# Encoder layer in one kernel: the decay products of the state-space part, from unrounded 128-column products to rounded two-part products of 128 and 64 columns

## Chip, cores and metric

The kernel runs on one core of a Trainium2 chip. The time is the device time of one execution in microseconds (us); below, a run is one such execution and the median of several is given. Less is better.

## What is computed

One encoder layer over 256 tokens of width 2048: a combined input projection, three branches (a bidirectional state-space scan, a dilated window attention, a convolution module), their gated sum, an output projection and an MLP. The change touches the state-space branch alone, and in it the product that the reference calls `y_diag`, in chunks of 128 tokens, 32 heads of 64 channels, 4 groups of 8 heads, in both directions:

```python
lmat = jnp.exp(jnp.where(lower, seg, -jnp.inf))
cb = jnp.einsum("bclgn,bcsgn->bgcls", cc, bc)
y_diag = jnp.einsum("bgrcls,bcsgrp->bclgrp", cb[:, :, None] * lmat, xdt)
...
y = y_fwd + y_bwd + d_skip[:, None] * xh
```

For one chunk and one head this is a 128x128 matrix (decay times `cb` times `dt`, both directions added) times a 128x64 block of x.

## The kernel before

**The stream of weights.** All large products are cut into blocks of up to 512 output columns, and each block into units of 256 rows of its weight. There are 696 units, counted here from 0. For unit k, SyncE loads a tile `raw`, ScalarE (ACT) rounds it to `hi` (L1211), VectorE (DVE) forms the rest `lo` (L255), and TensorE (PE) multiplies `hi` and `lo` with the two parts of the activations into a PSUM tile `main` (L1264 to L1276). `hi` and `lo` have four buffers each, `raw` five, `main` two. The loop at the end of the kernel issues, for each k, the split of unit k+3, then the products of unit k, then whatever side work fits in.

**Side work.** Everything else is a job: a generator that says before each step what it needs. "v", "a", "g" and "p" are planned nanoseconds on DVE, ACT, GpSimd and PE; "b" is a PSUM bank (of 4); "m" asks for slabs, the 4 KB-per-partition tiles that all jobs share (`SLOTS`, 33 of them); "w" lets some units pass; "j" waits for another job's result. `Sched.tick` gives each engine some planned time per unit, and jobs are tried in order of priority: 0 for those that read a `main` and so free it, 1 for conv and output parts, 2 for attention, 3 for the state-space jobs (`job_cb`, `job_ssd`), 4 for the long convolution. A job that asks for slabs that aren't free waits.

**What forces an order.** Before the first product of a block, `mm` asks `S.require` that the block two before it has been read, since there are two `main` tiles. If it hasn't, `require` runs jobs without regard to planned time, by rising priority, until it has:

```python
S.require(lambda: id(j) in st["main_free"], f"block {bi - 2} read")
...
for j in [x for x in self.jobs if x.prio <= level]:
    while not cond() and not j.done and self._try(j, True):
        moved = True
```

All that these jobs issue then stands, on every engine, ahead of the block's first unit. In the program before this happens once, at unit 28, with two steps.

**The state-space jobs.** `job_ssd(g, c)` serves 8 heads of group g and chunk c; there are eight such jobs, and two of a group can be open at once. It takes four slabs: `rh`, `rl` (the masked decay increments, rounded and rest), `em` and `xsx`. After an off-diagonal part (L811 to L825) it goes twice through a half of four heads. A half issues, in this order: masks scaled by the increments on ACT and DVE (L832, L835), four products that sum them (L842), `cb` scaled by dt (L846, L854), the exponential (L849), their product (L857), the head products (L864) and the addition to `y` (L869). L864 takes x for two heads at once, so of its 128 columns the half that belongs to the other head is thrown away by the strided read at L867.

Of the kernel before, what the change touches and what calls it, by code (L numbers as in the profile page):

```python
# [12 lines left out]
F32 = mybir.dt.float32  # L13
F32R = mybir.dt.float32r
BF16 = mybir.dt.bfloat16
AF = mybir.ActivationFunctionType
ALU = mybir.AluOpType
# [3 lines left out]
P = 128  # L21
# [169 lines left out]
def kernel(ctx: ExitStack, tc: tile.TileContext, xT, xn, par, cm, cd, cq, w1, wq, ws, out):  # L191
    nc = tc.nc
    S = Sched()
# [11 lines left out]
    def nm(s):  # L205
        cnt[0] += 1
        return f"{s}_{cnt[0]}"

    def slab(shape, dt=F32, name="s"):
        return gp.tile([P] + list(shape), dt, tag="g", name=nm(name))  # L210

    def bank(shape=(512,), name="b"):
        return pd.tile([P] + list(shape), F32, tag="d", name=nm(name))
# [4 lines left out]
    V, A, G, PE = nc.vector, nc.scalar, nc.gpsimd, nc.tensor  # L218
# [11 lines left out]
    def par_(k, i=0, n=1):  # L230
        o = _OFF[k][0] + i
        return cpar[:, o:o + n]
# [563 lines left out]
    def job_ssd(g, c):  # L796

        yield "j", lambda: cbs[g] is not None
        dt, adh, adl, sp = st["dt"], st["adh"], st["adl"], st["sp"]
        yield "m", 4  # L800
        rh = slab([2, 4, P], F32R, name="rh")
        rl = slab([2, 4, P], F32R, name="rl")
        em = slab([2, 4, P], name="em")
        xsx = slab([2, 512], name="xsx")
        cb, x, yy = cbs[g], xs[g], y[g][:, c, :]
        o = 1 - c
        sS = sp[:, 0 if c == 1 else 2, 8 * g:8 * g + 8]
        sP = sp[:, 1 if c == 1 else 3, 8 * g:8 * g + 8]
        v8 = lambda ap: ap.rearrange("p (h e) -> p h e", h=8)
        yield "v", 620  # L810
        V.tensor_tensor(v8(xsx[:, 0, :]), v8(x[:, o, :]), sS[:, :, None].to_broadcast([P, 8, 64]), op=ALU.mult)  # L811
        yield "g", 1200
        G.tensor_tensor(v8(xsx[:, 1, :]), v8(x[:, c, :]),
                        par_("dsk", 8 * g, 8)[:, :, None].to_broadcast([P, 8, 64]), op=ALU.mult)
        yield "b", 1
        bo = bank()
        yield "w", 1
        yield "p", 860
        PE.matmul(bo, cb[:, 4 + c, :], xsx[:, 0, :], start=True, stop=True)  # L819
        yield "w", 1  # L820
        yield "v", 620
        V.tensor_tensor(v8(yy), v8(bo), sP[:, :, None].to_broadcast([P, 8, 64]), op=ALU.mult)
        S.banks += 1
        yield "v", 620
        V.tensor_tensor(yy, yy, xsx[:, 1, :], op=ALU.add)  # L825
        for hb in range(2):
            for d in range(2):
                for i in range(4):
                    col = 32 * d + 8 * g + 4 * hb + i
                    msk = LE if d == 0 else GE  # L830
                    yield "a", 290
                    A.activation(rh[:, d, i, :], msk, AF.Copy, scale=adh[:, c, col:col + 1].bitcast(F32))  # L832
                col = 32 * d + 8 * g + 4 * hb
                yield "v", 620
                V.tensor_tensor(rl[:, d], msk[:, None, :].to_broadcast([P, 4, P]),  # L835
                                adl[:, c, col:col + 4][:, :, None].to_broadcast([P, 4, P]), op=ALU.mult)
            yield "w", 1
            yield "b", 1
            ba = bank((4, P))
            yield "p", 900  # L840
            for n, (lt, src) in enumerate(((gtr, rh[:, 0]), (gtr, rl[:, 0]), (ltr, rh[:, 1]), (ltr, rl[:, 1]))):
                PE.matmul(ba, lt, src, start=(n == 0), stop=(n == 3))  # L842
            for i in range(4):
                yield "a", 290
                col = 8 * g + 4 * hb + i
                A.activation(em[:, 1, i, :], cb[:, c, :], AF.Copy, scale=dt[:, c, col:col + 1])  # L846
            yield "w", 1
            yield "a", 500
            A.activation(em[:, 0], ba, AF.Exp)  # L849
            S.banks += 1  # L850
            for i in range(4):
                yield "v", 270
                col = 32 + 8 * g + 4 * hb + i
                V.scalar_tensor_tensor(em[:, 1, i, :], cb[:, 2 + c, :], dt[:, c, col:col + 1], em[:, 1, i, :],  # L854
                                       op0=ALU.mult, op1=ALU.add)
            yield "v", 620
            V.tensor_tensor(em[:, 0], em[:, 0], em[:, 1], op=ALU.mult)  # L857
            yield "w", 1
            yield "b", 1
            bd = bank((4, P))  # L860
            yield "p", 880
            for i in range(4):
                pr = 256 * hb + 128 * (i // 2)
                PE.matmul(bd[:, i, :], em[:, 0, i, :], x[:, c, pr:pr + P], start=True, stop=True)  # L864
            yield "w", 1
            yield "v", 400
            bv = bd.rearrange("p (q r) e -> p q (r e)", q=2).rearrange("p q (s e) -> p q s e", s=4)[:, :, 0::3, :]  # L867
            yv = yy[:, 256 * hb:256 * hb + 256].rearrange("p (q s e) -> p q s e", q=2, s=2)
            V.tensor_tensor(yv, yv, bv, op=ALU.add)  # L869
            S.banks += 1  # L870
        S.give(4)
        st["ssd_c"][g] += 1
        st["ssd_n"] += 1
        if st["ssd_c"][g] == 2:
            S.give(2)
            if g == 3:
                S.give(2)
# [242 lines left out]
    def xbc_block(i):  # L1120
        def post(m):
            js = [(job_xbc(m, i, (16, 20, 0, 4, 8, 12)[i]), 1)]
            if i >= 2:
                js += [(job_cb(i - 2), 3), (job_ssd(i - 2, 0), 3), (job_ssd(i - 2, 1), 3)]
            return js
        block("W", "h", post)
# [37 lines left out]
    for o in ORDER:  # L1164
        k, i = o[0], int(o[1])
# [235 lines left out]
```

## Time and profile before

| what | value |
|---|---|
| median of 3 runs | 1981.73 us (1981.35 to 1984.19) |
| the profiled execution | 1983.86 us |
| its span | 1982.1 us |
| DVE busy | 1309.0 us, 66% of the span |
| ACT busy | 1036.0 us, 52% of the span |
| granted TensorE clock, mean | 0.999 |
| state-space halves on the chip | first L842 at 298.5 us, last L869 at 741.1 us |

The profile page gives the busy time of each engine, then groups of instructions by source line; a group's row says what it writes and reads, how often it ran, its busy time, the mean time of one, and how long its engine sat idle before it and for whom. PE is one queue of products with a queue of weight loads (PEld) beside it. A PE product's listed time includes its way through the array, so products overlap; what one costs is read from the distance of two starts.

### The profile page before, as it was taken

The page shows a single profiled execution, that of the slowest core. Times are in us where ns is not written, and L with a number is a line of the kernel's source. Part 1 is how long each engine was busy: PE and PEld are TensorE (multiplying, and loading weights), DVE is VectorE, ACT ScalarE, POOL GpSimd, SP SyncE. Part 2 cuts the span into 40 slices and gives each one's busy share as a digit, 9 for nine tenths or more (in the row PEclk, how much of TensorE's full clock was granted, in tenths as well). Part 3 has the DMA queues.
Part 4 walks back from the last instruction along what each step waited for, and adds up shares of the span by engine and source line. Part 5 has one row for each costly group of instructions (what it writes and reads, how often), then busy time and mean ns, then how long its engine had stood idle before and what let it go on. Part 6 is the DMA issues. An engine that isn't in the chain of part 4 may idle for free.

```text
span 1982.1 us, 29949 instructions
## 1 busy us (share of the span) xinstructions
PE 1966.0 (99%) x11798; PEld 1766.0 (89%) x11798; DVE 1309.0 (66%) x1847; ACT 1036.0 (52%) x1446; POOL 47.5 (2%) x42
## 2 busy tenths in 40 slices
PE   8999999999999999999999999999999999999999
PEld 7999999999998888888888888999988998998887
DVE  5778887887887889896654555555555554455443
ACT  6654576777757655545654444544443443344332
POOL 0000010000000000003000000000000000000000
PEclk9999999999999999999999999999999999999999
DMA  8555554554554555555555556555555555555554
GB/s 284 184 175 183 165 185 145 167 172 144 184 170 161 176 181 178 183 191 187 190 191 183 189 189 207 194 186 192 188 190 189 189 191 191 188 186 191 190 181 149
DMA packets 105342, 364.51 MB, mean 184 GB/s; under 512 B 11760, under 2 KB 12272, under 8 KB 105200
## 3 DMA queue, kind: packets, MB, share of 16 engines
q1 hardware_dynamic: 103904, 360.23, 55.4%
q10 hardware_dynamic: 1296, 2.36, 0.3%
q8 instruction: 92, 1.51, 0.3%
q14 instruction: 50, 0.41, 0.1%
HBM read 360.45 MB, written 2.10 MB: 183 GB/s over the span
## 4 chain that ended last, share of the span: by engine, by line
PE 95%; DVE 0%; issue 0%
PE main L1273 19%; PE main L1274 19%; PE main L1276 19%; PE main L1266 11%; PE main L1264 11%; PE main L1268 11%; PE b L842 1%; PE b L864 1%; PE b L968 1%; PE b L1273 0%; PE b L1274 0%; PE b L1276 0%; PE b L819 0%; PE b L501 0%; PE b L757 0%; PE b L742 0%
## 5 line engine op out<-in xcount | busy, mean ns | idle before, releaser
L255 DVE TENSOR_TENSOR lo<-raw,hi 128x1024 fp32r<-128x1024 f32 (+2 forms) x697 | 831.5, 1194 | 643.5 <-ACT hi L1211 638.7
L1211 ACT ACTIVATE hi<-raw 128x1024 fp32r<-128x1024 f32 (+2 forms) x695 | 716.2, 1032 | 868.7 <-PE main L1274 487.8
L1273 PE MATMUL main<-hi,hh 128*128 128x512 f32 (+1 forms) x800 | 306.1, 383 | 0.0
L1274 PE MATMUL main<-hi,hl 128*128 128x512 f32 (+1 forms) x800 | 299.0, 374 | 0.0
L1266 PE MATMUL main<-x2l,hi 128*128 128x256 f32 x1024 | 246.4, 281 | 0.0
L1264 PE MATMUL main<-x2h,hi 128*128 128x256 f32 x1024 | 246.3, 279 | 0.0
L1266 PE MATMUL main<-hl,hi 128*128 128x256 f32 x896 | 216.3, 281 | 3.2 <-DVE hl L255 3.2
L1264 PE MATMUL main<-hh,hi 128*128 128x256 f32 x896 | 217.7, 282 | 0.0
L565 DVE SCALAR_TENSOR_TENSOR co<-cin,cpar,co 128x256 f32<-128x256 f32 x480 | 211.1, 491 | 0.0
L1276 PE MATMUL main<-lo,hh 128*128 128x512 f32 (+1 forms) x800 | 200.5, 372 | 0.0
L1264 PEld LDWEIGHTS main<-x2h,hi 128*128 128x128 f32 x1024 | 192.7, 188 | 0.2
L1266 PEld LDWEIGHTS main<-x2l,hi 128*128 128x128 f32 x1024 | 192.6, 188 | 0.2
L1273 PE MATMUL main<-hi,ah 128*128 128x512 f32 x480 | 188.9, 394 | 0.0
L1274 PE MATMUL main<-hi,al 128*128 128x512 f32 x480 | 188.6, 393 | 0.0
L1273 PEld LDWEIGHTS main<-hi,hh 128*128 128x128 f32 x800 | 152.5, 191 | 23.4 <-ACT hi L1211 1.2
L1274 PEld LDWEIGHTS main<-hi,hl 128*128 128x128 f32 x800 | 152.2, 190 | 22.9 <-issue 1.9
L1266 PEld LDWEIGHTS main<-hl,hi 128*128 128x128 f32 x896 | 168.8, 188 | 4.2 <-DVE hl L255 3.6
L1264 PEld LDWEIGHTS main<-hh,hi 128*128 128x128 f32 x896 | 169.2, 189 | 0.6
L1276 PEld LDWEIGHTS main<-lo,hh 128*128 128x128 f32 x800 | 148.0, 190 | 22.1
L1268 PE MATMUL main<-x2h,lo 128*128 128x256 f32 x1024 | 138.3, 277 | 0.0
L1276 PE MATMUL main<-lo,ah 128*128 128x512 f32 x480 | 130.1, 393 | 0.0
L1268 PEld LDWEIGHTS main<-x2h,lo 128*128 128x128 f32 x1024 | 127.6, 188 | 0.0
(244 smaller groups left out, 2304.5 us busy)
## 6 DMA issues: line engine op xcount, KB each, us to landing
raw<-ws_dram SPq DMA_DIRECT2D x600, 512.0 KB, 3.3
raw<-wq_dram SPq DMA_DIRECT2D x88, 384.0 KB, 3.1
raw<-w_dram SPq DMA_DIRECT2D x7, 448.0 KB, 7.0
xr<-xn_dram SPq DMA_DIRECT2D x4, 512.0 KB, 9.2
x<-xn_dram SPq DMA_DIRECT2D x4, 512.0 KB, 4.3
xt<-xT_dram SPq DMA_DIRECT2D x7, 256.0 KB, 7.0
out_dram<-x SPq DMA_DIRECT2D x4, 256.0 KB, 3.7
out_dram<-x ACTq DMA_DIRECT2D x4, 256.0 KB, 5.6
```

Source lines behind the costliest of these rows:

```text
L255: V.tensor_tensor(lo, raw, hi.bitcast(F32), op=ALU.subtract)
L565: V.scalar_tensor_tensor(dst[:, e, :], x[:, e, k:k + T], par_("dw", (2 * i + e) * 31 + k), dst[:, e, :], op0=ALU.mult, op1=ALU.add)
L842: PE.matmul(ba, lt, src, start=(n == 0), stop=(n == 3))
L864: PE.matmul(bd[:, i, :], em[:, 0, i, :], x[:, c, pr:pr + P], start=True, stop=True)
L968: PE.transpose(b[:, e, t * P:t * P + P], src[:, t, k * P:k * P + P], ID)
L1211: A.activation(h, r, AF.Copy)
L1264: PE.matmul(o, wh[:, e, cs], ah, start=(first and e == 0 and c % 2 == 0), stop=False, skip_group_check=True)
L1266: PE.matmul(o, wh[:, e, cs], al, start=False, stop=False, skip_group_check=True)
L1268: PE.matmul(o, wl[:, e, cs], ah, start=False, stop=(last and e == 1), skip_group_check=True)
L1273: PE.matmul(o, ah[:, xs_], wh[:, e, :], start=(first and e == 0), stop=False)
L1274: PE.matmul(o, al[:, xs_], wh[:, e, :], start=False, stop=False)
L1276: PE.matmul(o, ah[:, xs_], wl[:, e, :], start=False, stop=(last and e == 1))
```

## The change

The head products are no longer made from unrounded operands. x of the chunk is split once per job into a rounded part and a rest, which stand side by side per head in a new slab `xhl` (128 columns per head). The matrix `em` is split in the same way into `rh[:, 0]` and `rh[:, 1]`, the slab that held the masked increments until then. Per head there are two products in the rounded format: the rounded matrix with both parts of x (128 columns), and the rest of the matrix with the rounded part of x (64 columns). The product of the two rests is left out. The two column halves are then added to `y` one after the other. A job now asks for five slabs instead of four; the number of slabs stays 33.

```diff
-        yield "m", 4
+        yield "m", 5
+        xhl = slab([8, 2, 64], F32R, name="xhl")
...
+        yield "a", 500
+        A.activation(xhl[:, :, 0, :], v8(x[:, c, :]), AF.Copy)
+        yield "w", 1
+        yield "v", 620
+        V.tensor_tensor(xhl[:, :, 1, :], v8(x[:, c, :]), xhl[:, :, 0, :].bitcast(F32), op=ALU.subtract)
...
             yield "w", 1
+            yield "a", 500
+            A.activation(rh[:, 0], em[:, 0], AF.Copy)
+            yield "w", 1
+            yield "v", 620
+            V.tensor_tensor(rh[:, 1], em[:, 0], rh[:, 0].bitcast(F32), op=ALU.subtract)
+            yield "w", 1
             yield "b", 1
             bd = bank((4, P))
-            yield "p", 880
+            yield "p", 480
             for i in range(4):
-                pr = 256 * hb + 128 * (i // 2)
-                PE.matmul(bd[:, i, :], em[:, 0, i, :], x[:, c, pr:pr + P], start=True, stop=True)
+                PE.matmul(bd[:, i, :], rh[:, 0, i, :], xhl[:, 4 * hb + i].rearrange("p a e -> p (a e)"), start=(i == 0),
+                          stop=False, skip_group_check=True)
+                PE.matmul(bd[:, i, 0:64], rh[:, 1, i, :], xhl[:, 4 * hb + i, 0, :], start=False, stop=(i == 3),
+                          skip_group_check=True)
             yield "w", 1
-            yield "v", 400
-            bv = bd.rearrange("p (q r) e -> p q (r e)", q=2).rearrange("p q (s e) -> p q s e", s=4)[:, :, 0::3, :]
-            yv = yy[:, 256 * hb:256 * hb + 256].rearrange("p (q s e) -> p q s e", q=2, s=2)
-            V.tensor_tensor(yv, yv, bv, op=ALU.add)
+            yv = yy[:, 256 * hb:256 * hb + 256].rearrange("p (i e) -> p i e", i=4)
+            for a in range(2):
+                yield "v", 400
+                V.tensor_tensor(yv, yv, bd[:, :, 64 * a:64 * a + 64], op=ALU.add)
             S.banks += 1
-        S.give(4)
+        S.give(5)
```

The planner therefore sets the side work in another order. In the changed program, the jobs' free slabs fall to 0 at unit 120, 1 at unit 176 and 0 at unit 242, and at these places a job that has to read a `main` waits for slabs (or stands behind one that does), so `require` runs the state-space jobs to their end. The lines of the changed program are moved: L838 is L832 of before, L841 is L835, L848 is L842, L852 is L846, L855 is L849, L860 is L854, L863 is L857, L965 is L951, L1225 is L1211. New are L828 and L831 (the parts of x), L866 and L869 (those of the matrix), L875 and L877 (the products) and L883 (the two additions).

The first place is ACT between the units 179 and 181 of the changed program; unit 176 is the first of the block of attention values. `hi` is the rounded weight, `qn` the normalised queries, read from a `main`, and the numbers behind the names are the tiles' own. These are the last rows ahead of the rounding of unit 180:

```order
L866 ACTIVATE rh_5796<-em_5798 128x512
L828 ACTIVATE xhl_5884<-xs_5689 128x8x64
L838 ACTIVATE rh_5885<-cmask,adh 128x128 x8
L852 ACTIVATE em_5887<-cb_5786,dt 128x128 x4
L855 ACTIVATE em_5887<-b_5907 128x512
L866 ACTIVATE rh_5885<-em_5887 128x512
L838 ACTIVATE rh_5885<-cmask,adh 128x128 x8
L852 ACTIVATE em_5887<-cb_5786,dt 128x128 x4
L855 ACTIVATE em_5887<-b_5945 128x512
L866 ACTIVATE rh_5885<-em_5887 128x512
L489 ACTIVATE qn_5973<-main_5271,qrs_5479 128x128 x6
L1225 ACTIVATE hi_5998<-raw_5638 128x768
```

In the program before, ACT reads the same block's `main` in these rows:

```order
L1211 ACTIVATE hi_5756<-raw_5684 128x768
L459 ACTIVATE junk_5732,ss_5731<-main_5477 128x128 x2
L763 ACTIVATE oh_828<-b_5737 128x2x128
L1211 ACTIVATE hi_5783<-raw_5712 128x768
L270 ACTIVATE rs_803_5800<-qms_5774 128x6
L1211 ACTIVATE hi_5808<-raw_5754 128x768
L489 ACTIVATE qn_5829<-main_5477,qrs_5775 128x128 x4
L1211 ACTIVATE hi_5837<-raw_5781 128x768
```

What stood before between the roundings of many units now stands in one piece between those of units 179 and 180: after the rounding of unit 179 come six squares, two copies of x, seven copies of `em` (five of them with the masks, scaled copies and exponential of a whole half ahead of them), two parts of x, and last the six `qn`.

The second place is DVE around the units 242 to 250, where the attention's projections are multiplied by their gates (L965, before L951) and so read. In the changed program, after the forced half of a state-space job:

```order
L869 TENSOR_TENSOR rh_7787<-em_7789,rh_7787 128x512
L883 TENSOR_TENSOR y_6947<-y_6947,b_7864 128x256 x2
L255 TENSOR_TENSOR lo_7895<-raw_7748,hi_7894 128x1024
L255 TENSOR_TENSOR lo_7914<-raw_7769,hi_7913 128x1024
L965 TENSOR_TENSOR mg_7891<-main_7730,sg_6818 128x512 x2
L255 TENSOR_TENSOR lo_7935<-raw_7892,hi_7934 128x1024
L255 TENSOR_TENSOR lo_7954<-raw_7911,hi_7953 128x1024
L965 TENSOR_TENSOR mg_7910<-main_7878,sg_7028 128x512 x2
```

and before:

```order
L255 TENSOR_TENSOR lo_7727<-raw_7669,hi_7726 128x1024
L951 TENSOR_TENSOR mg_7715<-main_7675,sg_6761 128x512 x2
L854 SCALAR_TENSOR_TENSOR em_7503<-cb_6818,dt,em_7503 128x128
L255 TENSOR_TENSOR lo_7750<-raw_7697,hi_7749 128x1024
L854 SCALAR_TENSOR_TENSOR em_7503<-cb_6818,dt,em_7503 128x128 x3
L857 TENSOR_TENSOR em_7503<-em_7503 128x512
L255 TENSOR_TENSOR lo_7773<-raw_7724,hi_7772 128x1024
L951 TENSOR_TENSOR mg_7765<-main_7730,sg_6982 128x512 x2
```

Each `lo` row is the split of one unit. Before, the gate product of the block that ends with unit 241 stands behind the split of unit 245; now it stands behind that of unit 247, and those of the next two blocks have moved two splits back in the same way.

## Prediction

> **What bounds the kernel now.** First the page's head, then who waits for whom.
>
> ```profile
> span 1982.1 us, 29949 instructions
> PE 1966.0 (99%) x11798; PEld 1766.0 (89%) x11798; DVE 1309.0 (66%) x1847; ACT 1036.0 (52%) x1446; POOL 47.5 (2%) x42
> ```
>
> PE is busy 99% of the span. The list of waits, PE's own, has five rows in all:
>
> ```profile
> PE b L296 <- DVE dg L291: 4.1, 1, 4.1
> PE main L1266 <- DVE hl L255: 3.2, 2, 2.2
> PE main L1273 <- ACT hi L1211: 2.9, 2, 2.1
> PE b L1288 <- DVE ones L236: 1.1, 1, 1.1
> PE main L1273 <- ACT hi L1208: 0.7, 2, 0.3
> ```
>
> That is 12 us in the whole run. ACT, on the other hand, waits for PE to free a `hi` buffer:
>
> ```profile
> ACT hi L1211 <- PE main L1274: 487.8, 319, 2.6
> ```
>
> So the time is the sum of the PE products, plus whatever makes PE stop. Work added to ACT and DVE costs nothing as long as it stands between the splits. It costs its full length where PE has no product left that may go on.
>
> **The products themselves.** The timeline of PE around one group of L864, columns start and length:
>
> ```profile
> 306.00 1.11 PE L1268 MATMUL main<-hh,lo 128*128 128x256 f32 x8
> 306.94 1.05 PE L864 MATMUL b<-xs,em 128*128 128x128 f32 x8
> 307.75 0.36 PE L1264 MATMUL main<-hh,hi 128*128 128x256 f32 x1
> 307.96 0.28 PE L1266 MATMUL main<-hl,hi 128*128 128x256 f32 x1
> 308.08 0.28 PE L1264 MATMUL main<-hh,hi 128*128 128x256 f32 x1
> ```
>
> Four unrounded products are eight records. From 306.94 to 307.96 are 1.02 us, less one 256-column product of 0.12 (307.96 to 308.08): 0.90 us a group, 0.1125 a record; 16 groups take 14.4 us. The four decay products (rounded, 512 columns) of one half lie at
>
> ```profile
> 298.64 0.39 PE L842 MATMUL b<-rh,gtr 128*128 128x512 f32 x1
> ...
> 299.56 0.28 PE L1264 MATMUL main<-hh,hi 128*128 128x256 f32 x1
> ```
>
> which is 0.92 us, 0.23 each. The change makes 16 x 8 rounded records out of 16 x 8 unrounded ones, each with its own 128x128 weight load. No rounded product under 256 columns is in this trace. Lower bound: from 512 to 256 columns a rounded one falls from 0.23 to 0.12, so by that slope 128 and 64 columns take 0.06 and 0.03, a group 0.37, and 16 groups save 8.5 us. Upper bound: if narrow rounded products each cost a whole unrounded one (0.225), a group is 1.8 us and the change costs 14.4. I take the nearest row, a record with the same weight load and 128 columns: 0.1125 each, **difference 0**.
>
> The Trainium skill (TensorE: Matmul & The Clock Gate, LDWEIGHTS (loading the stationary operand)) puts a weight load at its columns over 1.2 GHz, 107 ns here, which speaks against this change; by it the difference is 0 as well, and the 0.1125 agrees. The same page (Weight-path perf modes — Fast Weight Load (FWL) and DoubleRow) lets a faster load go with types other than FP32; by that the lower bound would be near, and no row here decides it.
>
> **Where PE stops.** The order in the changed program has forced pieces ahead of the first units of nine blocks: 120, 176, 184, 192, 200, 242, 244, 246, 248. PE can't start such a unit before ACT or DVE has read the `main`, and these reads stand at the end of the piece. ACT can't begin a piece early: it stands behind the rounding of the unit three ahead, which waits for the unit before the stop. So the whole piece lies bare, less the PE work in it, which had to be done anyway. The prices, from ACT's and DVE's timeline and the groups by form:
>
> ```profile
> 299.31 1.28 ACT L849 ACT_TABLE_LOAD   x1
> 300.61 0.60 ACT L849 ACTIVATE em<-b 128x512 f32<-128x512 f32 x1
> 301.10 1.27 ACT L832 ACTIVATE rh<-cmask,adh 128x128 fp32r<-128x128 f32 x4
> 302.27 1.05 ACT L1211 ACTIVATE hi<-raw 128x1024 fp32r<-128x1024 f32 x1
> ```
>
> ```profile
> 301.08 1.13 DVE L854 SCALAR_TENSOR_TENSOR em<-cb,dt,em 128x128 f32<-128x128 f32 x4
> 302.31 0.69 DVE L857 TENSOR_TENSOR em<-em 128x512 f32<-128x512 f32 x1
> ```
>
> ```profile
> L835 DVE TENSOR_TENSOR rl<-cmask,adl 128x512 fp32r<-128x512 f32 x32 | 21.8, 684 | 0.0
> L869 DVE TENSOR_TENSOR y<-y,b 128x256 f32<-128x256 f32 x16 | 6.6, 414 | 0.0
> L819 PE MATMUL b<-xsx,cb 128*128 128x512 f32 x16 | 8.2, 591 | 0.0
> L972 ACT ACTIVATE mh<-b 128x512 fp32r<-128x512 f32 x8 | 4.8, 598 | 2.4 <-PE b L968 2.4
> L459 ACT ACTIVATE junk<-main 128x128 f32<-128x128 f32 x48 | 13.2, 274 | 3.0 <-DVE dtt L387 1.9
> L459 ACT ACTIVATION_READ_ACCUMULATOR junk<-main 128x1 f32 x48 | 9.4, 196 | 0.0
> L489 ACT ACTIVATE qn<-main,qrs 128x128 f32<-128x128 f32 x48 | 14.4, 375 | 15.1 <-DVE qrs L283 11.6 <-DVE qrs L482 3.5
> L657 ACT ACTIVATE xq<-main,cpar 128x256 f32<-128x256 f32 x24 | 12.2, 567 | 0.0
> L951 DVE TENSOR_TENSOR mg<-main,sg 128x512 f32<-128x512 f32 x8 | 5.1, 683 | 0.0
> L505 ACT ACTIVATE qkT<-b,qgs 128x512 f32<-128x512 f32 x4 | 2.8, 705 | 0.2 <-PE b L501 0.2
> L517 ACT ACTIVATE v<-main 128x384 f32<-128x384 f32 x6 | 2.6, 484 | 0.0
> L788 DVE TENSOR_TENSOR cb<-b,cmask 128x128 f32<-128x128 f32 x8 | 2.2, 280 | 0.0
> ```
>
> Four masks take 1.17 (301.10 to 302.27); the four scaled copies have their shape and get the same. The new copies of 512 go by L972 (0.60), as do ACT's other steps of 512; the new subtractions of 512 go by L835 (0.69), as do DVE's other steps of 512. One half, from one exponential to the next in the same job: L857 0.69, copy 0.60, subtraction 0.69, products 0.90 plus 0.17 until the last is out (1.05 listed for eight, last start to end), eight masks 2.34 (they overwrite `rh`, so they wait for the products), scaled copies 1.17, exponential 0.60: **7.2 us**. A half that opens a job goes through DVE instead: 3.05 as above to the products, two additions 0.83, L811 0.69, L819 0.59, L822, L825 and the new subtraction 2.07, two `rl` 1.37, the last two decay products 0.62, exponential 0.60: **9.8 us**.
>
> *Unit 176.* Opening: six squares with their read-outs 2.8, table load 1.28, root 0.2, two copies of x 1.2, scaled copies 1.17, table load 1.28, exponential 0.60: 8.5. Then two waiting halves follow each other: copy, subtraction, products, additions (3.2), two L854 0.57, L857 0.69, copy, subtraction, products 2.36, and masks, scaled copies, exponential 4.1: 10.9. Then a half that opens a group (9.8 and four mask products at 0.28, 1.1), a half in the same job (7.2), one that opens a job (9.8), one in the same job (7.2); last L857, copy and six `qn` 2.25: 3.5. Together 58. PE work in it: seven product groups, five decay groups, eight transposes (0.11 each) and four larger products (about 0.5 each), 6.3 + 4.6 + 0.9 + 2.0 = 13.8. **Lost: 44.**
>
> *Unit 120.* Table load, sigmoid 0.60, masks and scaled copies 2.34, table load, exponential, L857, copy, two copies of 0.60 and four L657: 10.9, less 2.7 of PE: **8.2**. *Unit 242.* Products to exponential of the job's first half 7.8, second half 7.2, L857 and copy 1.3, table load, two gates of 0.60: 18.8, less 5.1 of PE: **13.7**.
>
> *The small ones.* 184: L505 0.7, its half 0.5, six `qn` 2.25: 3.4. 192: 0.7, 0.5 and two L517: 2.2. 200: table load, sigmoid, two copies and four L657: 5.4. 244, 246, 248: round 1.05 and split 1.2 of the unit three ahead, two L951 1.37, less the four rounded products left (0.92): 2.7 each. **Sum 19.**
>
> **The clock.** PE's longest wait, 4.1 us, and what follows it, by windows (columns: busy PE, PEld, DVE, ACT, POOL; clock; DMA share; GB/s) and in PE's timeline:
>
> ```profile
> 40.00:44.00 4.00, 2.78 (x11) 2.60 (x12) 2.32 (x11) 2.26 (x10) 0.00 (x0) 0.67 0.55 145
> 44.00:48.00 4.00, 4.00 (x23) 4.00 (x22) 3.75 (x8) 1.05 (x3) 0.00 (x0) 0.91 0.51 178
> ```
>
> ```profile
> 42.16 1.91 PE L395 MATMUL b<-dtt,perm 128*128 128x128 f32 x8
> 43.73 0.67 PE L1273 MATMUL main<-hi,xgh 128*128 128x384 f32 x1
> ```
>
> The same eight records that L864 does in 0.90 took 1.57 here; the clock is lost for 4 x 0.33 + 4 x 0.09 = 1.7 us in all. At 176 PE works under a quarter of the time, so I take these longer records for the whole piece: seven groups at 0.67 more and five decay tails at 0.45 (half of 0.92): 7.0. At 242 three groups and two tails: 2.9. Behind 120, 176, 200 and 242, 1.7 each: 6.8. **Sum 16.7**; without it 0. The Trainium skill (TensorE: Matmul & The Clock Gate, What's actually happening) says that an idle window of some 3.4 us halves the clock and as long a busy one gives it back; this agrees with the 0.67 and 0.91, and by it the sum would be the same.
>
> **The sum.** 44 + 8.2 + 13.7 + 19 + 16.7 + 0 = **102 us** on the profiled execution of 1983.86; on the median, 2.1 below it, that gives **2083 us**. What else is added, 24 copies of 0.60 on ACT and 24 subtractions and 16 additions on DVE, 14.4 and 23 us, lies partly in these pieces and partly between splits, where ACT's 488 us of waiting for PE cover it; bare, all of it would be some 37.
>
> **Rivals.**
> *The clock stays up*, because the PE work within the pieces is enough to hold it: 102 - 17 gives 85, 2067 us. For it: a half has two spells of PE work in its 7.2 us, so no single wait need reach 4 us behind the opening. Against it: the clock fell after one wait of 4.1 us.
> *Narrow rounded products are quick* (0.37 a group): 8.5 less, 2075 us. For it: the rounded ones stream twice as fast per record. Against: same weight loads. The fast weight load of the Trainium skill (TensorE: Matmul & The Clock Gate, cited above) would give this.
> *They cost as much as unrounded ones*, so that the change doesn't do what it says: 14 more at most, 2097 us.
> *ACT and DVE are further ahead than I take them*, and the pieces lie beside PE's work: then only the products' difference is left, and with the products at their lower bound the time falls to about 1973 us. ACT's 488 us of waits speak for it. It decides from the point where ACT could start the piece at 176 58 us before PE's stop; the four `hi` buffers allow it one unit, about 2 us, and the piece's first rows read the `main` that has just been finished.
>
> **How the numbers follow.** Forecast 0.55, clock up 0.17, quick products 0.12, costly products 0.12, pieces hidden 0.04. All but the last are slower. Chains worked out by adding rows can be off by a fifth either way (hand-overs are left out, some steps may overlap): 17 on 85. Low end: clock up, quick products, chains a little shorter, 2045; high end: costly products and longer chains, 2115. A measurement tells 0.2% (4 us) from no change: faster 0.03, within 0.2% 0.02, slower 0.95.
>
> **What would show it.** In PE's list of waits, ACT and DVE rows of tens of us in place of 12; at the start of unit 176 one wait with `qn` (L489) as its releaser; slices with a granted clock under 1 and a low PE share near 500 to 570 us; L875 and L877 in steps of about 0.11 where the clock is full. ACT and DVE busy time grow by some 14 and 23 us, PE's hardly. The prediction is wrong if PE's waits stay near 12 us, if the piece at 176 is far from 58 us, or if a group of the new products takes 0.4 or 1.8 us at full clock.

## The result, and the profile after

| | before | after |
|---|---|---|
| median | 1981.68 us (1981.35 to 1984.19) | 2095.97 us (2095.76 to 2096.96) |
| after / before | | 1.0575, 95% interval 1.0557 to 1.0593 |
| profiled execution | 1983.86 us | 2096.96 us |
| granted TensorE clock, mean | 0.999 | 0.971 |

The change costs 114 us; 102 were forecast, with a range of 2045 to 2115 us for the time. The page of the changed kernel: span, busy times, and the strips of PE's busy share and granted clock in 40 slices of 52 us each.

```profile
span 2095.2 us, 30032 instructions
...
PE 2013.7 (96%) x11798; PEld 1794.2 (86%) x11798; DVE 1334.2 (64%) x1887; ACT 1052.4 (50%) x1470; POOL 42.3 (2%) x42
...
PE   8999999997599987999999999999999999999999
...
PEclk9999999998599997999999999999999999999999
```

The number of PE records is the same, 11798, and yet PE is busy for 47.7 us more. The same records last longer where the clock is halved, and the clock strip shows where: in the slices 9 and 10, counted from 0 (471 to 576 us), and in slice 15 (786 to 838 us). Only part of the loss is therefore listed as waiting. PE's list of waits (total us, times, longest), which had 12 us in five rows before, begins:

```profile
PE b L875 <- ACT rh L866: 29.6, 10, 9.4
PE b L848 <- DVE rl L841: 9.0, 8, 2.4
PE main L1287 <- DVE mg L965: 8.3, 3, 2.8
PE b L820 <- DVE xsx L812: 5.4, 3, 2.1
```

All 14 rows together hold 77 us. The rest of the loss hides in longer records. It is more plainly read from the distance of two starts on PE, from the last work of one unit to the first product of the next. At unit 176, in PE's timeline (start, length, then what the engine waited for):

```profile
501.11 0.86 PE L1290 MATMUL main<-lo,hh 128*128 128x384 f32 x4
501.80 1.03 PE L685 MATMUL b<-cmask,xq 128*128 128x128 f32 x8
...
568.81 0.47 PE L875 MATMUL b<-xhl,rh 128*128 128x128 f32 x1 [2.08 <-ACT rh L866]
...
571.05 0.67 PE L1287 MATMUL main<-hi,hh 128*128 128x384 f32 x1
```

From the first work behind unit 175's products (501.80) to unit 176's first product (571.05) are 69.25 us, with 13.8 us of PE work in them by the prediction's count. From 510 us on the windows (busy PE, PEld, DVE, ACT, POOL; clock; DMA share; GB/s) say

```profile
510.00:540.00 30.00, 14.96 (x38) 9.40 (x38) 16.45 (x38) 13.17 (x34) 1.05 (x1) 0.50 0.00 0
540.00:572.00 32.00, 18.51 (x49) 12.22 (x50) 17.48 (x38) 17.77 (x50) 0.00 (x0) 0.50 0.00 1
```

No engine is busy even 60% of that time, the clock is at 0.50 throughout, and the weights' DMA stands still (0.00, 0 to 1 GB/s), as no unit goes on and frees a buffer. That is one chain of dependent steps, with the rest of the chip waiting.

### The profile page after: what moved, and what is told of

Its sections match the earlier page's. It is cut to its first block, busy times and chain, and to the rows that moved or that the text cites. A ratio compares the mean times of both kernels' runs of the same rounds, so it can differ in the third digit from the quotient of the medians.

```text
span 2095.2 us, 30032 instructions
## 1 busy us (share of the span) xinstructions
PE 2013.7 (96%) x11798; PEld 1794.2 (86%) x11798; DVE 1334.2 (64%) x1887; ACT 1052.4 (50%) x1470; POOL 42.3 (2%) x42
## 4 chain that ended last, share of the span: by engine, by line
PE 60%; DVE 0%; issue 0%
PE main L1287 14%; PE main L1288 14%; PE main L1290 14%; PE main L1282 6%; PE main L1278 6%; PE main L1280 6%; PE b L982 1%; PE b L1287 0%; PE b L1290 0%; PE b L1288 0%; DVE x L1091 0%; DVE mg L965 0%; PE b L608 0%; PE b L296 0%; PE b L581 0%
## 5 line engine op out<-in xcount | busy, mean ns | idle before, releaser
L1225 ACT ACTIVATE hi<-raw 128x1024 fp32r<-128x1024 f32 (+2 forms) x695 | 715.9, 1032 | 937.6 <-PE main L1288 528.7
```

Source lines behind the costliest of these rows:

```text
L1225: A.activation(h, r, AF.Copy)
```

## Experiments

Two theories stood against each other. **The places**: the same arithmetic costs nothing as long as its steps stand between the units; what costs is that state-space jobs run short of slabs and are then run bare ahead of a unit, with the clock halved on top. **The work**: the longer half (two more steps in its chain, one more addition), or the new products, cost wherever they stand.

### The same arithmetic without forced pieces

Two edits to the changed kernel, and the second alone as a control on the kernel before:

```diff
-        yield "m", 5
-        xhl = slab([8, 2, 64], F32R, name="xhl")
+        yield "m", 4
...
         V.tensor_tensor(yy, yy, xsx[:, 1, :], op=ALU.add)
+        xhl = slab([8, 2, 64], F32R, name="xhl")
...
-        S.give(5)
+        S.give(4)
```

```diff
-SLOTS = 33
+SLOTS = 34
...
-    rp = ctx.enter_context(tc.tile_pool(name="rp", bufs=5))
+    rp = ctx.enter_context(tc.tile_pool(name="rp", bufs=4))
```

> The changed kernel's arithmetic whole, with the xhl slab taken only after the addition to yy (when xsx is dead, so that a job counts four slabs as before), and one slab more in the pool of slabs (34 for 33) against one buffer less in the pool rp (4 for 5). The planner's order of it has none of the long forced pieces ahead of units 120, 176, 184, 192, 200, 242, 244, 246 and 248. Theory (the forced pieces and the clock that they cost make all of the 114 us; the split products cost what the old ones did, and the added ACT and DVE work lies beside the matrix products): 1982 us, within 0.3% of before (1976 to 1988), no slice of granted clock under 0.9 between 340 and 900 us. Rival 1, the longer chain of a half costs by itself, in whatever order: the waits of the halves stay, about 16 halves x 2 us and more, 2010 us or over. Rival 2, the rounded products are quicker than the old ones: 1973 to 1976. Rival 3, they are dearer: 1990 to 1996.

> The kernel before with only the two buffer counts of the run beside it (34 slabs, 4 rp buffers), as its control. All theories: within 0.2% of before, 1978 to 1986 us. If it is slower by x, the run beside it is to be read against this one and not against before.

Measured: 1983.88 us against 1983.71 of before on that chip, ratio 1.0003 (0.9994 to 1.0012); the control 1981.32 us, 0.9993 (0.9984 to 1.0001). With every added instruction still there, the loss is gone against the kernel before; against the control, which has the same buffers, 2.6 of the 114 us are left, and no run says what they are. The page's strips of PE and clock without forced pieces:

```profile
PE   8999999999999999999999999999999999999999
...
PEclk9999999999999999999999999999999999999999
```

How the added steps are hidden shows in ACT's groups by line (busy us, mean ns | idle just before them, and for whom). First the changed kernel, then the one without pieces:

```profile
L866 ACT ACTIVATE rh<-em 128x512 fp32r<-128x512 f32 x16 | 10.0, 624 | 11.6 <-DVE em L863 11.6
L855 ACT ACTIVATE em<-b 128x512 f32<-128x512 f32 x16 | 9.6, 598 | 18.7 <-PE b L848 18.6
```

```profile
L866 ACT ACTIVATE rh<-em 128x512 fp32r<-128x512 f32 x16 | 10.0, 622 | 1.0 <-DVE em L863 1.0
L855 ACT ACTIVATE em<-b 128x512 f32<-128x512 f32 x16 | 9.5, 595 | 0.5 <-PE b L848 0.4
```

The same 16 roundings take the same 10 us. In the changed kernel ACT stands idle for 30 us in front of these two lines, since nothing else is queued between the steps of the chain. Without pieces the steps are spread over other units, and the idle time is 1.5 us. This rules out the second theory for all but those 2.6 us.

### What a product costs

Both kernels start from the one without pieces. One leaves the 64-column product out, that is, the rest of the matrix times the rounded x; the other widens it to 128 columns and so adds the product of the two rests:

```diff
-                          stop=False, skip_group_check=True)
-                PE.matmul(bd[:, i, 0:64], rh[:, 1, i, :], xhl[:, 4 * hb + i, 0, :], start=False, stop=(i == 3),
-                          skip_group_check=True)
+                          stop=(i == 3), skip_group_check=True)
```

```diff
-                PE.matmul(bd[:, i, 0:64], rh[:, 1, i, :], xhl[:, 4 * hb + i, 0, :], start=False, stop=(i == 3),
-                          skip_group_check=True)
+                PE.matmul(bd[:, i, :], rh[:, 1, i, :], xhl[:, 4 * hb + i].rearrange("p a e -> p (a e)"), start=False,
+                          stop=(i == 3), skip_group_check=True)
```

> As the run without pieces, and the product of 64 columns (rounded remainder of the matrix times the rounded x) is left out, 64 records in all. If each product costs its weight load of 0.1125 us whatever its width: 64 x 0.1125 = 7.2 us less than the run with both, and the start-to-start step of two L875 records falls from 0.225 to 0.11 us. If its columns were what it costs (512 columns take 0.22 us in the records of L848, so 64 take 0.03): 64 x 0.03 = 1.8 us less. If the products lie beside the waits of their chain: no change.

> As the run without pieces, but the second product of a head has 128 columns too (it adds the product of the two remainders). If the weight load is what a product costs: the same time within 0.1%, steps of 0.225 us for a pair as with 64 columns. If the columns cost: 64 x 0.03 = 1.8 us more by the rate of the 512-column records, and a pair's step over 0.25 us; if a 128-column product costs twice one of 64, 0.15 against 0.075 of the 0.225: 64 x 0.075 = 4.8 us more.

Measured: without the 64-column product 1978.79 us, 0.9975 (0.9963 to 0.9986). Against the run with both products that is 5.1 us less between the medians and 7.4 less between the spans of the profiled executions (1974.4 and 1981.8), where 7.2 were expected if each product costs its load and 1.8 if its columns cost. The times of one kernel differ by 2 to 4 us among themselves, so the steps on PE decide it. With 128 columns in both, 1982.97 us, 0.9997 (0.9988 to 1.0005). One group of four heads in PE's timeline, without the 64-column product, then with 128 and 128:

```profile
321.79 0.56 PE L875 MATMUL b<-xhl,rh 128*128 128x128 f32 x4
322.19 0.33 PE L1276 MATMUL main<-hh,hi 128*128 128x256 f32 x1
322.36 0.28 PE L1278 MATMUL main<-hl,hi 128*128 128x256 f32 x1
```

```profile
324.06 0.22 PE L875 MATMUL b<-xhl,rh 128*128 128x128 f32 x1
324.12 0.28 PE L877 MATMUL b<-xhl,rh 128*128 128x128 f32 x1
324.23 0.28 PE L875 MATMUL b<-xhl,rh 128*128 128x128 f32 x1
...
324.90 0.34 PE L1278 MATMUL main<-hh,hi 128*128 128x256 f32 x1
325.07 0.28 PE L1280 MATMUL main<-hl,hi 128*128 128x256 f32 x1
```

By the prediction's reading (to the second main product, less one of 0.12) the groups take 0.45 and 0.89 us. With 128 and 64 columns it is 0.90 (316.27 to 317.29 less 0.12, in the changed kernel), and before 0.90. So eight records are eight times 0.11, whether they have 64 or 128 columns and whether their operands are rounded or not. PE's weight loads in the changed kernel fit this; these rows are the queue PEld, where a load has 128 columns whatever its product:

```profile
316.16 0.19 PEld L875 LDWEIGHTS b<-xhl,rh 128*128 128x128 f32 x1
316.27 0.19 PEld L877 LDWEIGHTS b<-xhl,rh 128*128 128x128 f32 x1
316.39 0.19 PEld L875 LDWEIGHTS b<-xhl,rh 128*128 128x128 f32 x1
```

They start 0.11 us apart, one for each product, so the load is the likely limit. A least time per product, whatever it loads, would look the same, and no run here parts the two. The kernel without the 64-column product is quicker than both, but it is a less exact one, not the same computation done faster.

### Slabs and the planner

Three kernels whose forced pieces fall at other places. The first is the kernel before, in which a job only counts a fifth slab; the second the changed kernel with the late `xhl` of above and all buffers as they were; the third the changed kernel with one number of the planner changed.

```diff
-        yield "m", 4
+        yield "m", 5
...
-        S.give(4)
+        S.give(5)
```

```diff
-WPRIO = 1
+WPRIO = 4
```

> The kernel before, with its own products, steps and instructions, but a state-space job counts and gives back five slabs of the pool instead of four (the fifth is only counted, nothing is put in it). The planner then forces a piece of about four halves ahead of unit 144, one of about four halves ahead of unit 176, and a few steps ahead of unit 184. Theory (what costs is that the pool runs out and the jobs are then run to their end with TensorE waiting): an old half that runs alone lies near 6 us (7.2 us of the new one less the two steps of the split), of which 1.7 us are products, so two pieces of 22 - 6 = 16 us, 3 + 1.7 us of clock for each, 3 us at 184: about +44 us, 2010 to 2040 us. Rival (the longer half of the split is what costs, not the slab): within 0.5% of before, 1975 to 1993.

> The changed kernel whole, but xhl is taken after the addition to yy, when xsx is dead: a job counts four slabs as before. The planner still forces pieces, at other places: about one and a half halves ahead of unit 160, four ahead of unit 244, and a few steps ahead of units 246, 248 and 256. Theory (the price of a piece is its halves): 7 us at 160, 29 - 7 = 22 at 244, 3 x 4.2 = 12.6 at the small ones (by their price in the changed kernel), 3.4 us of warm-ups: +45 us, 2015 to 2045. Rival (the fifth slab is all that costs): 1976 to 1990.

> The changed kernel whole, five slabs to a job; only the planner's WPRIO is 4 for 1, so that state-space jobs (priority 3) no longer hold their steps back by the clock estimates. Its order has one forced piece, four groups of split products and three of decay sums ahead of unit 144, and none of the others. Theory (the price is that of the pieces alone): four halves at 7.2 us = 29 us less 6 us of products = 23, and 2 to 4 us of clock: 2003 to 2013 us, nine tenths of the way... that is, about 88 of the 114 us come back without any change of buffers or arithmetic. Rival (the split's own work costs in whatever order): 2030 us or over.

| | time, us | ratio to before, interval | expected over before | measured over before | long gaps on PE, us |
|---|---|---|---|---|---|
| fifth slab alone, old products | 2025.06 | 1.0207 (1.0190 to 1.0224) | 44 | 41 | 23.4, 23.7, 3.3 |
| four slabs, late `xhl` | 2041.60 | 1.0292 (1.0276 to 1.0307) | 45 | 58 | 12.9, 32.3, 3.1, 3.2, 3.2 |
| one piece | 2001.47 | 1.0091 (1.0076 to 1.0106) | 23 + 2 to 4 | 18 | 24.5 |

(Before on that chip: 1983.80 us. A gap is the distance between the starts of two main products that follow each other; side work within it is included.)

The fifth slab alone, with not one instruction of the split, costs 41 us: a shortage of slabs is enough. But it isn't the slab alone. With four slabs per job pieces remain, and 58 us are lost; probably the longer half keeps its slabs longer, which no run shows by itself. And the number of slabs doesn't fix the loss: with five slabs and all of the new arithmetic, one number of the planner gives back some 95 of the 114 us (2001.47 against 2095.97). The sizes of the last two forecasts were off, by 13 and by some 8 us: in the second kernel the two large pieces lose 10.2 and 25.2 us (12.9 and 32.3 less 2.7 and 7.1 of PE work) where I had 7 and 22, which is half of the 13; the other half isn't placed. In the third, the first of the four product groups was ready at once and cost no chain. Its PE timeline:

```profile
403.73 0.22 PE L875 MATMUL b<-xhl,rh 128*128 128x128 f32 x1
...
411.68 0.48 PE L875 MATMUL b<-xhl,rh 128*128 128x128 f32 x1 [2.08 <-ACT rh L866]
...
428.01 0.56 PE L1278 MATMUL main<-hh,hi 128*128 128x256 f32 x1
```

The old half in the pieces of the first kernel, two product groups in PE's timeline:

```profile
417.42 2.05 PE L864 MATMUL b<-xs,em 128*128 128x128 f32 x8 [1.51 <-DVE em L857]
...
423.73 2.05 PE L864 MATMUL b<-xs,em 128*128 128x128 f32 x8 [1.50 <-DVE em L857]
```

It takes 6.31 us from group to group. The new half in the changed kernel takes 7.73 (below), also at half clock. So the split makes a bare half 1.4 us longer; the bare run itself is the larger part of the price.

### The clock held up

The changed kernel in its own order, with products on a constant ahead of the real ones wherever the planner forces steps (`S.forcing` is set while `require` runs jobs):

```diff
...
+    def warmup(b):
+        for _ in range(7 if S.forcing else 0):
+            PE.matmul(b, dist[:, 0, 0:P], dist[:, 1, :], start=True, stop=True)
...
+            warmup(ba.rearrange("p i e -> p (i e)"))
             for n, (lt, src) in enumerate(((gtr, rh[:, 0]), (gtr, rl[:, 0]), (ltr, rh[:, 1]), (ltr, rl[:, 1]))):
...
+            warmup(bd.rearrange("p i e -> p (i e)"))
             for i in range(4):
```

> The changed kernel whole and in its own order; wherever the planner forces steps, seven products of 512 bfloat16 columns of a constant are put ahead of the four products of the decay sums and ahead of the eight products of a half, into the same bank, which the real ones then overwrite (147 in all; nothing reads them). Theory (the chain of a half sets the pieces, and the halved clock adds to it): the clock stays at 1 in the middle of the pieces of 176 and 242, the 69 us piece falls by 7 to 12 us, the 22 us piece by 3 to 5, and the slower records behind both go (1.7 us each): 2072 to 2084 us. Rival 1, the clock doesn't set anything there: no change, 2090 to 2100. Rival 2, the clock falls all the same: each group of seven then takes 7 x 0.43 = 3 us, longer than the 2 us waits that it stands in, and the time is 2100 to 2115.

Measured: 2084.33 us, 1.0509 (1.0494 to 1.0525), 11.6 us less than the changed kernel, just above the 2072 to 2084 us that were expected. (The two were timed beside different runs of the kernel before, 1983.80 and 1981.68 us; taken over those, the gain is 13.8 us.) Windows of the run with the clock held:

```profile
510.00:540.00 30.00, 22.27 (x82) 11.99 (x84) 17.65 (x41) 14.78 (x40) 1.05 (x1) 0.77 0.00 1
540.00:564.00 24.00, 18.33 (x84) 9.94 (x85) 16.79 (x36) 15.42 (x47) 0.00 (x0) 1.00 0.00 0
```

The clock is up in the second half of the piece at 176, and the piece still lasts 61 us (502.08 to 563.00, 60.92). The piece at 242 goes from 22.0 to 20.2, the one at 120 from 10.2 to 9.5. In the first half of the piece at 176 the clock fell twice all the same: it is 0.51 from 511.7 to 518.6 us, around a wait of 6.33 us on PE, and 0.50 from 528.8 to 535.6, around one of 1.66 us. The clock is thus a small part of the price, as far as this run held it up, and the chain of the half is most of the rest. Two halves of one job, from product group to product group, first in the changed kernel and then with the clock held:

```profile
540.78 0.47 PE L875 MATMUL b<-xhl,rh 128*128 128x128 f32 x1 [2.07 <-ACT rh L866]
...
548.50 0.47 PE L875 MATMUL b<-xhl,rh 128*128 128x128 f32 x1 [2.07 <-ACT rh L866]
```

```profile
538.14 0.33 PE L884 MATMUL b<-xhl,rh 128*128 128x128 f32 x1 [0.55 <-ACT rh L874]
...
544.60 0.33 PE L884 MATMUL b<-xhl,rh 128*128 128x128 f32 x1 [0.56 <-ACT rh L874]
```

7.72 us at half clock, 6.46 at the full one (L884 is L875 of the changed kernel, L874 its L866). Adding PE work made the kernel faster, because it stood in waits and kept the rest of the records short.

## Why the prediction was right

**The products.** Taken at a difference of 0, by the nearest row, and that held: 0.90 us a group before and after; the two runs on the product show that each record costs 0.11 us whatever its columns, the distance of two weight loads. Both rivals on it (0.37 and 1.8 us a group) are out. The faster load for types other than FP32, which the Trainium skill (TensorE: Matmul & The Clock Gate, Weight-path perf modes — Fast Weight Load (FWL) and DoubleRow) describes, doesn't show in the rounded format: its loads start 0.11 us apart. That agrees with the section LDWEIGHTS (loading the stationary operand) on the same page of the Trainium skill, by which 128 columns are estimated at 107 ns.

**The pieces.** The step that carried the forecast, that everything forced ahead of a unit lies bare, is shown by the run without pieces. Unit by unit, the loss from start to start less the PE work that the prediction counted, from PE's timeline of the changed kernel:

| place | forecast, chain + clock within it | measured |
|---|---|---|
| 120 | 8.2 | 7.4 (10.06 less 2.7) |
| 176 | 44 + 7.0 = 51 | 55.4 (69.25 less 13.8) |
| 242 | 13.7 + 2.9 = 16.6 | 16.7 (21.76 less 5.1) |
| 184, 192, 200, 244, 246, 248 | 19 | some 16 |
| clock coming back behind the places | 6.8 (4 x 1.7) | some 15.6 (6 x 1.7, 2 x 2.7) |
| sum | 102 | some 111 |

Of the 113.1 us between the two profiled executions some 111 are placed, but not to the last us. The rest of the kernel differs, too. In the MLP the splits of units 341 and 694, with no state-space work between them, are 988.5 us apart before and 994.9 after. In the run without pieces it is 992.7 and with the fifth slab alone 989.0, so it varies by several us from one profiled execution to the next, and I don't put it down to the change.

**The chain at 176**, term by term. The ends of its exponentials in ACT's timeline (start and length) mark the halves (the rows between are left out):

```profile
511.10 0.60 ACT L855 ACTIVATE em<-b 128x512 f32<-128x512 f32 x1
524.23 0.60 ACT L855 ACTIVATE em<-b 128x512 f32<-128x512 f32 x1 [0.64 <-PE b L848]
538.74 0.60 ACT L855 ACTIVATE em<-b 128x512 f32<-128x512 f32 x1 [2.71 <-PE b L848]
546.46 0.60 ACT L855 ACTIVATE em<-b 128x512 f32<-128x512 f32 x1 [0.64 <-PE b L848]
559.04 0.60 ACT L855 ACTIVATE em<-b 128x512 f32<-128x512 f32 x1 [6.57 <-PE b L848]
566.77 0.60 ACT L855 ACTIVATE em<-b 128x512 f32<-128x512 f32 x1 [0.64 <-PE b L848]
```

The steps are 13.13, 14.51, 7.72, 12.58 and 7.73 us; the prediction had 10.9, 10.9, 7.2, 9.8 and 7.2 at full clock, 46.0 against 55.67. With the clock held the last three are 6.4, 10.4 and 6.4. So the half in the same job was put 0.8 too high, the half that opens a job 0.6 too low, and the clock takes 1.3 to 2.2 us per half: each half pays for the slower decay sums, too, which I had charged only with the last two. The whole piece with the clock mostly held is 61 us for 58 forecast at full clock. The size was off by a twentieth, the mechanism wasn't. Some of that closeness is luck, since the errors of the single halves have both signs and partly cancel.

**The clock.** Forecast was a loss at 176, 242, 120 and 200; it came at 176, 242, 120, and not at 200, but at 184, 192, 244, 246 and 248. This is the mis-sized term: the return of the clock was priced at four places and 6.8 us, and is paid at eight, with some 15.6. Behind 176 and 242 it takes longer than the 1.7 us allowed: the clock stays at 0.50 until some 5.4 us after the first product of the unit (0.82 over the 4 us from 575 on leaves 1.4 us of them at 0.50), which costs 2.7. Windows behind 176 (start 571.05), behind 192 (start 620.63) and within the wait at 200:

```profile
571.00:575.00 4.00, 4.00 (x14) 4.00 (x14) 0.84 (x2) 0.84 (x1) 0.00 (x0) 0.50 0.01 4
575.00:579.00 4.00, 4.00 (x21) 4.00 (x21) 1.81 (x2) 0.85 (x1) 0.00 (x0) 0.82 0.39 128
...
620.00:626.00 6.00, 5.37 (x32) 5.37 (x33) 0.71 (x2) 1.64 (x3) 0.00 (x0) 0.72 0.26 88
...
646.00:650.00 4.00, 1.17 (x9) 0.92 (x8) 2.03 (x6) 3.97 (x6) 0.00 (x0) 1.00 0.58 183
```

The rival that the clock stays up is out. The run that held it gives a price for the part that it held: 11.6 us in all, of which 8.3 at 176 (69.25 to 60.92).

**The small places.** 200 was put at 5.4 and took 2.9 (3.11 less a usual distance of 0.2): the chain there began before PE stopped. 184, 192, 244, 246, 248 came within 0.7 of their forecast.

**What should have shown, and didn't.** A wait at unit 176 with `qn` as its releaser. There is none: the last `qn` ends at 570.30 (1.64 us from 568.66), while PE's own queue holds the last product group, forced ahead of the unit, until 571.05. The place was right, and the last step was PE's. Nor did PE's busy time stay: 47.7 us more, the longer records. ACT and DVE grew by 16.4 and 25.2 us, near the 14 and 23.

## What to carry to other kernels

In a kernel that is bound by one engine through a planner, the price of an edit isn't its instructions but where the planner puts them: look for the places where a resource (slabs here) falls to nothing and a step is forced, and price the chain of one bare piece, clock included. More steps between the units were free; the same steps in pieces cost 114 us, and an unchanged kernel that only counted one slab more lost 41. In this kernel a product with weights of its own costs 0.11 us with 64 or 128 columns, and 0.12 with 256, so for products this narrow count the records, not the columns.

## What the hardware showed that I had not expected

A wait of 1.90 us was enough to halve the clock (unit 192: clock 0.72 on the mean of the 6 us behind it), while one of 2.83 us at unit 200 wasn't (1.00). The length of a wait alone doesn't decide it. The mean of 0.72 over 6 us is that of one fall to 0.50 for some 3.4 us, which costs the 1.7. And PE needn't be idle to stay slow: from 510 to 572 us it was given 0.50 throughout, with its records, at that clock, listed as busy for 50% and 58% of the two windows. Seven constant products in each of its waits held it at 1.00 over the last 24 us of the same piece, listed as busy for 76% of the time. The step from product to product doubles at half clock: a pair of L875 and L877 takes 0.43 us in the piece (562.04 to 562.47) and 0.22 at full clock (316.42 to 316.64).
